# First layer's seven-product projection on one Trainium2 core: sums in the accumulation banks, weight sums on DVE at fixed steps, a written order on every engine, heads turned six steps later

## The chip, the cores and the metric

The kernel runs on one core of a Trainium2 chip. The core has a matrix engine (PE, with its own queue for loading weights, PEld), a vector engine (DVE), an activation engine (ACT), a general-purpose engine (POOL) and a synchronisation engine (SP) from which DMAs are issued; ACT can issue DMAs too. Each engine takes its instructions in the order in which they stand in its queue and waits at semaphores for the others. The metric is the device time of one execution in microseconds (us), less is better.

## What is computed

A two-layer decoder trunk over 1024 tokens of width 1024. The first layer is dilated sliding-window attention, the second a gated linear recurrence; both also attend to 256 memory tokens. The part that matters here is the first layer's input projection, its norms and its rotation:

```python
h = rms_norm(x, norm_gain[l])
cols = h @ w_in_a[j]                       # 1024 tokens x (9 x 1024 + 512 + 1536) columns
qkv = cols.reshape(B, S, 3, N_GROUPS, A_HEADS, HEAD_DIM)
q = rms_norm(qkv[:, :, 0], q_gain[:, None, :])
k = rms_norm(qkv[:, :, 1], k_gain[:, None, :])
v = qkv[:, :, 2]
q = apply_partial_rotary(q, cos5, sin5)    # the first 32 of 128 numbers of a head
k = apply_partial_rotary(k, cos5, sin5)
...
p = jnp.exp(s - m)                         # attention in windows, three dilations
o = jnp.einsum('brchqk,brckhd->brcqhd', p.astype(v.dtype), vc)
```

All of it is float32.

## The kernel before

**Tiling.** The 9 x 1024 columns of q, k and v are nine groups (line 851): for the dilations g = 2, 1, 0 in this order, k, v and q. A group is a product of 1024 tokens by 1024 inputs with 1024 inputs by 1024 columns. It is cut into halves both ways and done with seven products of 512 x 512 x 512 instead of eight (Winograd's form of Strassen's algorithm). The sides made of tokens are the quarters a11, a12, a22 and the sums s1 to s4 (line 852), turned once before and kept as a rounded high part and a rest (`hhi`, `hlo`, `s2hi` and so on). The sides made of weights are the quarters 11, 12, 21, 22 of the group's weights and sums of them.

**A product** (`product`, line 970) has four tiles of 128 tokens by 512 columns. A tile is 12 matmuls: four blocks of inputs, each with high x high, high x low and low x high (lines 983 to 985). Here one such tile is called a step; a group has 28 steps, the stage 252. Before, each tile had its own bank of PSUM (`acc`, three banks, and `po`, one), and all sums over products were made outside: by DVE from bank and SBUF (lines 993, 1000, 1004, 1005, 1008, 1011), one on POOL (line 1001), with copies out of the bank by ACT in three products (line 169).

**Weights.** `load` (line 856) brings halves of a quarter, 512 KB each, into raw tiles; `combine` (line 880) makes the sums in place, six on DVE and two on POOL per group (line 881); `split_side` (line 869) makes the rounded high half on ACT (`wh`) and the rest on DVE (`wl`, line 877), one product ahead, into a ring of four. `weights_ahead` (line 883) says after which tile of which product all this is issued.

**Heads.** A finished tile of q or k (16 per group) holds four heads of 128 tokens. `projected` (line 940): ACT squares it (946), DVE reduces (948) and adds the epsilon (176), POOL takes the power -0.5 (178), DVE scales (950), and POOL rotates (915, 917 twice, 919). Four ticks later (three for one tile) `spill_heads` (line 954) has PE turn the four heads (313), ACT takes them out of the bank with the gain (961), and a DMA on ACT's queue stores them to `qk_scr` (963, 967). Tiles of v are stored as they are.

**Order.** A scheduler orders the instructions of each engine; in this stage `with pinned()` (line 1040) holds PE's in program order, and only PE's. Loads are issued by SP, stores by ACT (line 108).

**Behind the stage** come the gates of the memory columns (`gate_mem`, lines 1088 and 1091), the memory's norm and projections, and the attention. There a loop over heads and tiles does scores, probabilities (DVE and ACT, tile `pa`, three buffers), turns them on PE (1157) and multiplies with the values (1170); a tile is turned one tile after its scores.

## Time and profile before

| | us |
|---|---|
| median of three timed runs | 2260.11 (2257.26, 2260.11, 2260.25) |
| the profiled execution's own time | 2256.34 |
| its span, first to last instruction | 2254.5 |
| busy in the span: PE | 2110.3 |
| DVE | 1307.1 |
| ACT | 852.4 |
| POOL | 596.4 |

TensorE's mean granted clock in the profiled execution is 0.977 of full speed. The profile names an instruction by engine, line of the kernel, operation and tiles (output <- inputs). "Idle before" is the time in which an engine waited just ahead of an instruction, and "<-" names what ended that wait. Busy times are sums over an engine; which of them sets the end is read from a stretch of the span and from who waits for whom. The seven-product stage reaches from the first matmul of line 983 at 73.9 us to about 929 us.

### The profile page before, as it was taken

Reading aid. Unit: us, or ns where it says so; the run is one execution under the profiler, and the core shown is the slowest. Engines: PE = TensorE matmul, PEld = TensorE weight load, DVE = VectorE, ACT = ScalarE, POOL = GpSimd, SP = SyncE. Lnnn points to the kernel's source line nnn. Section 1 sums busy time; section 2 is a strip of 40 time slices with the busy share of each in tenths; the row PEclk is TensorE's granted clock in tenths of the full one; section 3 lists DMA queues with packets and bytes.
Section 4 is the critical chain, followed back from the end, with each engine's and each line's share of the span. In section 5 each row is a group of like instructions: output and inputs, shape, how many; then the busy total and the mean of one; then the engine's idle time right before and its main releaser. Section 6 shows DMA issues by size and latency. Waiting matters only on the chain.

```text
span 2254.5 us, 29624 instructions
## 1 busy us (share of the span) xinstructions
PE 2110.3 (94%) x10713; PEld 1752.2 (78%) x10713; DVE 1307.1 (58%) x2546; ACT 852.4 (38%) x1599; POOL 596.4 (26%) x718
## 2 busy tenths in 40 slices
PE   7899988899888998899879999999999999999999
PEld 5677866778666786678768788888888888888887
DVE  7765557565676656555545755442557772777443
ACT  6544235352353423444655533232542322222211
POOL 2553155541566415402100630001310000000221
PEclk9999999999999999999999999999999999999999
DMA  6465356444343332642677847432111111212633
GB/s 185 122 102 100 112 100 78 98 103 126 84 86 106 109 121 82 208 150 61 212 259 239 269 142 257 151 121 73 57 57 48 57 48 50 73 47 88 221 121 112
DMA packets 416449, 272.50 MB, mean 121 GB/s; under 512 B 220448, under 2 KB 344624, under 8 KB 414256
## 3 DMA queue, kind: packets, MB, share of 16 engines
q1 hardware_dynamic: 155808, 189.72, 27.4%
q10 hardware_dynamic: 260496, 80.89, 14.4%
q8 instruction: 85, 1.39, 0.3%
q14 instruction: 60, 0.49, 0.1%
HBM read 187.60 MB, written 82.97 MB: 120 GB/s over the span
## 4 chain that ended last, share of the span: by engine, by line
PE 71%; DVE 9%; DMA 7%; POOL 5%; ACT 4%; issue 3%; ACTq 1%; SPq 0%; DVEq 0%; POOLq 0%
PE acc L983 6%; PE acc L984 6%; PE acc L985 6%; PE acc L495 5%; PE acc L496 5%; PE acc L497 5%; PE acc L600 4%; PE acc L601 4%; PE acc L602 4%; PE acc L255 4%; PE acc L254 4%; PE acc L253 4%; PE pt L313 2%; POOL rr L178 2%; PE s L1143 1%
## 5 line engine op out<-in xcount | busy, mean ns | idle before, releaser
L178 POOL TENSOR_TENSOR rr<-rv,nhalf 128x4 f32<-128x4 f32 (+1 forms) x150 | 155.8, 1041 | 842.9 <-DVE rv L176 841.8
L169 ACT ACTIVATE wh<-raw 128x1024 fp32r<-128x1024 f32 x206 | 217.0, 1058 | 284.4 <-PE acc L985 76.6
L877 DVE TENSOR_TENSOR wl<-raw,wh 128x1024 fp32r<-128x1024 f32 x126 | 158.1, 1258 | 175.3 <-ACT wh L169 175.2
L983 PE MATMUL acc<-wh,hhi 128*128 128x512 f32 x504 | 208.6, 414 | 0.2 <-ACT x L169 0.2
L984 PE MATMUL acc<-wl,hhi 128*128 128x512 f32 x504 | 201.7, 400 | 1.2 <-DVE wl L877 1.2
L985 PE MATMUL acc<-wh,hlo 128*128 128x512 f32 x504 | 201.0, 399 | 0.0
L496 PE MATMUL acc<-hlo,wh 128*128 128x512 f32 x480 | 191.4, 399 | 0.0
L497 PE MATMUL acc<-hhi,wl 128*128 128x512 f32 x480 | 191.2, 398 | 0.0
L495 PE MATMUL acc<-hhi,wh 128*128 128x512 f32 x480 | 190.1, 396 | 0.0
L215 DVE TENSOR_TENSOR wl<-raw,wh 128x1024 fp32r<-128x1024 f32 x80 | 100.2, 1254 | 119.3 <-ACT wh L169 117.8
L255 PE MATMUL acc<-wh,hlo 128*128 128x512 f32 x384 | 151.3, 395 | 5.8 <-DVE hlo L274 5.8
L253 PE MATMUL acc<-wh,hhi 128*128 128x512 f32 x384 | 150.6, 397 | 0.8 <-ACT wh L169 0.8
L254 PE MATMUL acc<-wl,hhi 128*128 128x512 f32 x384 | 151.2, 394 | 0.0
L600 PE MATMUL acc<-wh,yhi 128*128 128x512 f32 x360 | 144.4, 403 | 0.5 <-ACT yhi L169 0.5
L601 PE MATMUL acc<-wl,yhi 128*128 128x512 f32 x360 | 142.8, 397 | 0.0
L602 PE MATMUL acc<-wh,ylo 128*128 128x512 f32 x360 | 141.5, 398 | 0.0
L983 PEld LDWEIGHTS acc<-wh,hhi 128*128 128x128 f32 x504 | 98.8, 196 | 21.0 <-ACT x L169 2.3
L985 PEld LDWEIGHTS acc<-wh,hlo 128*128 128x128 f32 x504 | 97.9, 194 | 21.6
L984 PEld LDWEIGHTS acc<-wl,hhi 128*128 128x128 f32 x504 | 98.5, 196 | 20.4 <-DVE wl L877 1.6
L1148 ACT ACTIVATE pa<-pa,st 128x128 f32<-128x128 f32 (+1 forms) x192 | 84.5, 441 | 69.8 <-DVE st L1146 33.2
L881 POOL TENSOR_TENSOR raw<-raw 128x1024 f32<-128x1024 f32 x18 | 50.7, 2818 | 208.5 <-DVE raw L881 172.7
L496 PEld LDWEIGHTS acc<-hlo,wh 128*128 128x128 f32 x480 | 90.2, 188 | 16.9
(342 smaller groups left out, 5046.8 us busy)
## 6 DMA issues: line engine op xcount, KB each, us to landing
raw<-in_w_in_a_dram SPq DMA_DIRECT2D x106, 512.0 KB, 3.9
raw<-in_w_in_b_dram SPq DMA_DIRECT2D x40, 512.0 KB, 3.8
o_scr<-os ACTq DMA_DIRECT2D x96, 128.0 KB, 4.7
qk_scr<-c ACTq DMA_DIRECT2D x36, 256.0 KB, 4.1
raw<-in_w_mem_kv_dram SPq DMA_DIRECT2D x16, 512.0 KB, 4.1
kT<-qk_scr SPq DMA_DIRECT2D x8, 1024.0 KB, 5.5
qT<-qk_scr SPq DMA_DIRECT2D x8, 1024.0 KB, 8.7
vv<-v_scr SPq DMA_DIRECT2D x8, 1024.0 KB, 8.3
```

What stands on the lines that cost most here:

```text
L253: T.matmul(ps, hi, wh[:, j, :], start=at == 0, stop=False)
L254: T.matmul(ps, hi, wl[:, j, :], start=False, stop=False)
L255: T.matmul(ps, lo, wh[:, j, :], start=False, stop=at == n - 1)
L495: T.matmul(ps[:], wh[:, k, :], mh, start=k == 0, stop=False)
L496: T.matmul(ps[:], wh[:, k, :], ml, start=False, stop=False)
L497: T.matmul(ps[:], wl[:, k, :], mh, start=False, stop=k == 7)
L600: T.matmul(pss[ch][:], hi[:, k, :], wh[:, j, :], start=first and k == 0, stop=False)
L601: T.matmul(pss[ch][:], hi[:, k, :], wl[:, j, :], start=False, stop=False)
L602: T.matmul(pss[ch][:], lo[:, k, :], wh[:, j, :], start=False, stop=end and k == 3)
L983: T.matmul(flat, hi, wh, start=kt == 0, stop=False)
L984: T.matmul(flat, hi, wl, start=False, stop=False)
L985: T.matmul(flat, lo, wh, start=False, stop=kt == 3)
```

## The change

Seven things are changed.

1. The products stand in another order and add up in the banks: each of a tile's four banks takes products 0, 2, 3 and 4 one upon the other, then products 5 and 6; only product 1 has banks of its own (the two of `pS`). What a later sum needs is copied out between two products (`emptied`).
2. All weight sums are made by DVE, at fixed steps (`sums_`); half of quarter 21 and all of 22 are loaded a second time (`21r`, `22r`).
3. High and low halves of a side are made at separate steps (`split_high`, `split_low`).
4. A tile passes through fixed steps: `emptied` and `spread` one step behind its matmuls, `normed` three, `flip` (PE's transposes) six (`BEHIND`), `spill_heads` seven.
5. `pinned` holds PE, DVE, ACT, POOL and SP in program order. Stores of heads and of v are issued by SP instead of ACT.
6. Tiles have new names: rooms m, u and w, four of each, in place of x, y and c.
7. The last heads are finished between and behind the first gate of the memory columns. In the attention a tile's probabilities are turned two tiles after its scores, with four buffers `pa`.

```diff
-        SIDE = ("a12", "a11", "s1", "s2", "s3", "a22", "s4")
+        SIDE = ("a11", "a12", "s2", "s3", "a22", "s1", "s4")
+        FROM = ("11", "21", "22", "11", "21", "12", "22r")
...
         def combine(gi, out, a, b, h):
-            (G if out == "21'" else V).tensor_tensor(raws[gi, out, h], raws[gi, a, h], raws[gi, b, h], op=OP.subtract)
+            V.tensor_tensor(raws[gi, out, h], raws[gi, a, h], raws[gi, b, h], op=OP.subtract)
...
+            first, second = (1, 0) if p == 0 else (0, 1)
+            sums_ = {(0, 0): ("12", "12", "11", 0), (0, 1): ("12", "12", "11", 1), (0, 2): ("22", "22", "12", 0),
+                     (1, 0): ("22", "22", "12", 1), (1, 3): ("11", "22", "11", 0), (2, 0): ("11", "22", "11", 1),
+                     (2, 3): ("21", "21", "22", 0), (3, 0): ("21r", "21r", "22", 1)}
+            if i in (0, 1):
+                split_high(n + 1, (first, second)[i])
+            if i in (1, 2):
+                split_low(n + 1, (first, second)[i - 1])
+            if (p, i) in sums_:
+                out, a, b, h = sums_[p, i]
+                combine(gi, out, a, b, h)
+            for at, what in (((0, 2), ((0, "22", 1),)), ((2, 2), ((0, "21r", 1),)), ((2, 3), ((1, "11", 0),)),
+                             ((3, 0), ((0, "22r", 0),)), ((3, 1), ((0, "22r", 1),)), ((4, 2), ((1, "11", 1),)),
+                             ((4, 3), ((1, "12", 0), (1, "12", 1), (1, "21", 0))), ((5, 2), ((1, "22", 0),)),
+                             ((5, 3), ((1, "21", 1),))):
...
+        def matmuls(k, hook=None):
+            n, i = divmod(k, 4)
+            p = n % 7
+            if p in (0, 5):
+                banks[i] = bank(i)
+            ps = pS.tile([128, 4, 128], F32, name="s")[:] if p == 1 else banks[i]
...
+                T.matmul(flat, hi, wh, start=kt == 0 and p in (0, 1, 5), stop=False, **on)
+                T.matmul(flat, hi, wl, start=False, stop=False, **on)
+                T.matmul(flat, lo, wh, start=False, stop=kt == 3, **on)
...
+            if p in (0, 2, 3):
+                return
+            Q, m = {1: (0, i), 4: (0, 4 + i), 5: (1, 4 + i), 6: (1, i)}[p]
+            to = (ms, None, None, None, None, vs, us)[p - 1 if p == 1 else p]
+            if p != 4:
+                V.tensor_tensor(to[i], to[i], ps, op=OP.add)
+                c = to[i]
+            else:
+                ms[i] = c = room(f"m{i}")
+                copy(A, c, ps)
+            if i_ == 2:
+                Y.dma_start(tile_of(v_scr[g], m)[:, Q * 512:(Q + 1) * 512], c.rearrange("p h d -> p (h d)"))
+                return
...
+        def step(k, fill=None):
+
+            n, i = divmod(k, 4)
+            if k <= LAST:
+                sums_at[k] = matmuls(k)
+            spill_heads(k - 1 - BEHIND)
+            if k - 1 in sums_at:
+                emptied(k - 1, sums_at.pop(k - 1))
+            normed(k - 3)
+            if k <= LAST:
+                weights_ahead(n, i)
+                if i == 3 and n % 7 == 0 and groups[n // 7][0] != 2:
+                    group_tables(*groups[n // 7])
+            if fill:
+                fill()
+            spread(k - 1)
+            flip(k - BEHIND)
...
+        for k in range(LAST + 1):
+            with pinned(E.PE, E.DVE, E.Activation, E.Pool, E.SP):
+                step(k, {LAST - 2: lambda: ahead(1), LAST - 1: lambda: ahead(2)}.get(k))
...
+        step(LAST + 1)
+        gate_mem(MG0[0], between=lambda: [step(LAST + k) for k in (2, 3, 4)])
+        for k in range(5, BEHIND + 3):
+            step(LAST + k)
...
-                p = ap_.tile([128, 2, 256], F32, name="pa", bufs=3)
+                p = ap_.tile([128, 2, 256], F32, name="pa", bufs=4)
...
-                        old = turn_(*scored.pop()) if scored else None
+                        old = turn_(*scored.pop(0)) if len(scored) > 1 else None
```

Three places show how the instructions move on the engines. The first is DVE at the seam where the fourth group begins (k of the second dilation). `wl` is the low half of a side, `raw` a half of a quarter of the weights, `rc` and `rs` the group's rotation tables, `m`, `u`, `c` and `y` tiles of heads, `rr` the factor of the norm. Before:

```order
L950 TENSOR_TENSOR y3_2463<-y3_2463,rr4_2976 128x512
L924 TENSOR_TENSOR rc_693<-turns_126,gr_125 128x256
L927 SCALAR_TENSOR_TENSOR rs_694<-turns_126,gr_125 128x8x16 x2
L877 TENSOR_TENSOR wl_3124<-raw_2580,wh_3123 128x1024
L881 TENSOR_TENSOR raw_2580<-raw_3018,raw_2580 128x1024
L877 TENSOR_TENSOR wl_3128<-raw_2582,wh_3127 128x1024
L881 TENSOR_TENSOR raw_2490<-raw_2580,raw_2490 128x1024
L993 TENSOR_TENSOR c_3105<-x0_3008,acc_3092 128x512
L881 TENSOR_TENSOR raw_2582<-raw_3020,raw_2582 128x1024
L993 TENSOR_TENSOR c_3144<-x1_3044,acc_3131 128x512
```

and after:

```order
L1008 TENSOR_TENSOR u2_2374<-u2_2374,rr4_2854 128x512
L889 TENSOR_TENSOR wl_2926<-raw_2700,wh_2886 128x1024
L893 TENSOR_TENSOR raw_2562<-raw_2562,raw_2529 128x1024
L1008 TENSOR_TENSOR u3_2398<-u3_2398,rr4_2893 128x512
L889 TENSOR_TENSOR wl_2958<-raw_2564,wh_2924 128x1024
L893 TENSOR_TENSOR raw_2662<-raw_2662,raw_2560 128x1024
L930 TENSOR_TENSOR rc_691<-tabs_124 128x256
L933 SCALAR_TENSOR_TENSOR rs_692<-tabs_124 128x8x16 x2
L893 TENSOR_TENSOR raw_2961<-raw_2961,raw_2562 128x1024
L980 TENSOR_TENSOR m0_2915<-m0_2915,s_2993 128x512
L889 TENSOR_TENSOR wl_3038<-raw_2662,wh_3010 128x1024
```

The new group's sums (L893) and low halves now stand between the last scalings of the group before (L1008), ahead of the tables, where before the sums came behind the last heads of the group before.

The second place is SP's queue around the same seam: loads of `raw` and, after, the stores of heads to `qk_scr`. Before:

```order
L864 DMA raw_3022<-in_w_in_a_dram 128x2x512
L864 DMA raw_2721<-in_w_in_a_dram 128x2x512
L864 DMA raw_2723<-in_w_in_a_dram 128x2x512
L864 DMA raw_3018<-in_w_in_a_dram 128x2x512
L864 DMA raw_3020<-in_w_in_a_dram 128x2x512
```

and after:

```order
L1031 DMA qk_scr02_94<-w3_2481 128x32x16
L869 DMA raw_2961<-in_w_in_a_dram 128x2x512
L1031 DMA qk_scr02_94<-u0_2317 128x32x16
L1031 DMA qk_scr02_94<-u1_2342 128x32x16
L1031 DMA qk_scr02_94<-u2_2374 128x32x16
L1031 DMA qk_scr02_94<-u3_2398 128x32x16
L869 DMA raw_3186<-in_w_in_a_dram 128x2x512
```

The loads of block 22's second half (raw_2961) and of the second copy of 21's (raw_3186) now stand among stores of the group before.

The third place is ACT inside a group of q: squares of tiles of heads (into `s`), turned heads taken out of the bank `pt`, and, before, their stores. Before (q of the second dilation, products 4 to 6):

```order
L961 ACTIVATE c_4790<-pt_4915 128x4x32x4
L967 DMA qk_scr01_93<-c_4790 128x16x32
L946 ACTIVATE s_4900<-os_4897 128x512
L961 ACTIVATE c_4835<-pt_4963 128x4x32x4
L967 DMA qk_scr01_93<-c_4835 128x16x32
L946 ACTIVATE s_4936<-x0_4408 128x512
```

and after (q of the third dilation, products 4 to 6):

```order
L989 ACTIVATE s_2587<-m3_2585 128x512
L172 ACTIVATE wh_2596<-raw_2403 128x1024
L989 ACTIVATE s_2618<-w0_2424 128x512
L172 ACTIVATE wh_2627<-raw_2430 128x1024
L989 ACTIVATE s_2651<-w1_2451 128x512
L1025 ACTIVATE m0_2497<-pt_2670 128x4x16x8
L989 ACTIVATE s_2691<-w2_2467 128x512
L1025 ACTIVATE m1_2523<-pt_2708 128x4x16x8
```

The stores have left ACT's queue, and between a tile's square and its leaving the bank stand six steps instead of three or four: `m0` leaves after the square of `w1`, while before the first `c` left ahead of the square of `os`, the fourth tile of its product.

276 lines of the change are left out of this document (123 added, 153 removed).

## The prediction

> **What bounds the kernel now.** I read the stretches by engine first, then who PE waits for, then the pace of its matmuls. From the page's first line and the table of stretches (us; per engine busy us and instructions; then TensorE's granted clock, DMA share, GB/s):
>
> ```profile
> span 2254.5 us, 29624 instructions
> 74.00:929.00 855.00, 772.39 (x3417) 621.90 (x3416) 526.12 (x703) 335.82 (x426) 395.50 (x529) 0.96 0.44 103
> 1100.00:1300.00 200.00, 173.69 (x1156) 150.88 (x1155) 114.20 (x502) 114.53 (x416) 37.72 (x34) 0.95 0.80 263
> 1300.00:2254.50 954.50, 949.58 (x5064) 803.38 (x5063) 515.48 (x1055) 271.06 (x496) 103.48 (x93) 1.00 0.32 101
> ```
>
> The first stretch is the nine groups of seven products, which the change rewrites; the second is the attention of layer A, where it edits two lines. After 1300 PE is busy 949.6 of 954.5 us, and nothing there changes. So whatever can be won lies in PE's 83 idle us (855.0 - 772.4) of the first stretch and its 26 of the second, and in the clock below 1.00 there. Who PE waits for between 80 and 1000 us (total us, times, longest):
>
> ```profile
> PE pt L313 <- DVE rv L176: 43.1, 6, 7.4
> PE pt L313 <- POOL c L919: 18.4, 13, 3.1
> ```
>
> PE hardly waits for weights; it waits, in program order, in front of a tile's transposes (L313), whose heads are not yet scaled and rotated. The timeline shows PE's pace without such a wait, and after one:
>
> ```profile
> 301.37 0.39 PE L983 MATMUL po<-wh,hhi 128*128 128x512 f32 x1
> 304.10 0.39 PE L983 MATMUL acc<-wh,s2hi 128*128 128x512 f32 x1
> 311.80 0.40 PE L983 MATMUL acc<-wh,s2hi 128*128 128x512 f32 x1
> 326.26 0.40 PE L985 MATMUL po<-wh,s3lo 128*128 128x512 f32 x1
> 329.57 1.12 PE L313 MATMUL pt<-ident,c 128*128 128x128 f32 x4 [2.91 <-POOL c L919]
> 330.91 0.63 PE L984 MATMUL acc<-wl,hhi 128*128 128x512 f32 x1
> 331.34 0.63 PE L985 MATMUL acc<-wh,hlo 128*128 128x512 f32 x1
> 334.31 0.60 PE L313 MATMUL pt<-ident,c 128*128 128x128 f32 x4
> 334.67 0.48 PE L983 MATMUL acc<-wh,hhi 128*128 128x512 f32 x1
> 334.99 0.39 PE L984 MATMUL acc<-wl,hhi 128*128 128x512 f32 x1
> ```
>
> A step (one tile of one product, 12 matmuls) takes 304.10 - 301.37 = 2.73 us with a side from hhi, and 12 x (311.80 - 304.10)/33 = 2.80 us with a summed side. Four transposes add 0.45 us: the second matmul behind them starts at 334.99 instead of 334.31 + 0.23. After an idle gap of 2.91 us matmuls start 0.43 us apart, not 0.23: a wait costs more than its own length.
>
> **The floor of this stage.** Of 252 steps 144 have an hhi side and 108 a summed one, before and after: 144 x 2.73 + 108 x 2.80 = 695.5 us, and 96 tiles of q and k are turned: 43.2. That is 739 us. Measured are 855, of which some 13 matmuls of the gate behind the stage take 3: an excess of 113 us. The three v groups turn no heads, so it lies in the six q and k groups, about 19 us each: some 103 us a group instead of 84.5.
>
> **The change part by part.** The durations (min/median/max in ns for the first rows; count, busy us and mean ns for the last five), from the lines and groups of this stage:
>
> ```profile
> L877 DVE TENSOR_TENSOR wl<-raw,wh x126: 1210/1225/2316, 71.6 to 898.2; 128x1024 fp32r<-128x1024 f32 x126
> L881 DVE TENSOR_TENSOR raw<-raw x54: 1210/1225/3424, 83.5 to 848.8; 128x1024 f32<-128x1024 f32 x54
> L881 POOL TENSOR_TENSOR raw<-raw x18: 2361/2822/3313, 88.8 to 857.9; 128x1024 f32<-128x1024 f32 x18
> L950 DVE TENSOR_TENSOR c<-c,rr x36: 679/693/941, 100.7 to 900.5; 128x512 f32<-128x512 f32 x36
> L948 DVE TENSOR_REDUCE ss<-s x96: 676/684/693, 96.6 to 931.9; 128x4 f32<-128x512 f32 x96
> L176 DVE TENSOR_SCALAR rv<-ss x150: 138/164/555, 5.7 to 2106.5; 128x4 f32<-128x4 f32 x132, 128x1 f32<-128x1 f32 x18
> L178 POOL TENSOR_TENSOR rr<-rv,nhalf x150: 550/1011/2050, 6.0 to 2109.5; 128x4 f32<-128x4 f32 x132, 128x1 f32<-128x1 f32 x18
> L915 POOL TENSOR_TENSOR t<-c,rc x36: 446/460/789, 101.6 to 901.3; 128x128 f32<-128x128 f32 x36
> L917 POOL TENSOR_TENSOR t<-x,rs x48: 311/320/330, 159.7 to 919.4; 128x64 f32<-128x64 f32 x48
> L919 POOL TENSOR_TENSOR c<-t,t x36: 451/458/1433, 104.1 to 903.2; 128x128 f32<-128x128 f32 x36
> L1001 POOL TENSOR_TENSOR y<-y,x 128x512 f32<-128x512 f32 x36 | 54.7, 1523 | 125.6 <-DVE x L1000 110.0 <-issue 15.6
> L1008 DVE TENSOR_TENSOR x<-x,acc 128x512 f32<-128x512 f32 x32 | 21.8, 682 | 12.1 <-PE acc L985 12.0
> L169 ACT ACTIVATE wh<-raw 128x1024 fp32r<-128x1024 f32 x126 | 132.5, 1057 | 174.8 <-PE acc L985 76.6 <-PE po L985 64.3 <-issue 24.9
> L169 ACT ACTIVATE x<-acc 128x512 f32<-128x512 f32 x63 | 37.7, 599 | 108.3 <-DVE c L993 65.6 <-PE acc L985 31.7 <-DVE wl L877 4.8
> L961 ACT ACTIVATE c<-pt,gqk 128x512 f32<-128x512 f32 x18 | 18.3, 1015 | 27.1 <-PE pt L313 24.2 <-POOL t L917 2.9
> ```
>
> *Sums in the banks.* A group's 24 DVE additions become 12 (0.68 us each: 8 us less DVE); POOL loses four additions (4 x 1.5) and two weight sums (2 x 2.8), 12 us. DVE gains those two sums (2.5 us), ACT four copies out of a bank (2.4 us). PE's matmuls stay the same in number. A q or k group then asks of DVE 14 x 1.23 (low halves) + 8 x 1.23 (sums) + 12 x 0.68 + 16 x (0.69 + 0.68 + 0.16) = 60 us, of POOL 16 x (1.01 + 0.46 + 2 x 0.32 + 0.46) = 41, of ACT 14 x 1.06 + 32 x 0.60 + 16 x 1.02 = 50. PE needs 84.5. No engine is the bound by its sum.
>
> *New waits on the banks.* A bank is read one step after its product and written again four or more steps later: at least three steps, 8.2 us, cover a read of 0.6 to 0.7. The second product uses two other banks in turn, so there the addition must be done within the next step, 2.7 us. Cost nothing, unless DVE runs more than about 2 us late there.
>
> *Heads turned six steps behind.* From the end of a tile's matmuls its chain is addition 0.68, square 0.60, reduction 0.68, 0.16, power 1.01, scaling 0.69, rotation 1.56: 5.4 us. Between the tile and its transposes now stand five whole steps, 13.7 us at the least. The waits of 43.1 and 18.4 us go as long as DVE and POOL are less than 8 us behind. What is late next is DVE at the seam of two groups. From the sixth product's second step to the next group's third, ten steps, DVE has scalings, low halves and three sums on top of POOL's rotations.
>
> *DVE against POOL.* Two neighbours of the timeline show how much they exclude each other:
>
> ```profile
> 88.78 3.31 POOL L881 TENSOR_TENSOR raw<-raw 128x1024 f32<-128x1024 f32 x1 [10.88 <-DVE raw L881]
> 89.75 3.42 DVE L881 TENSOR_TENSOR raw<-raw 128x1024 f32<-128x1024 f32 x1
> 366.20 1.00 POOL L178 TENSOR_TENSOR rr<-rv,nhalf 128x4 f32<-128x4 f32 x1
> 366.30 1.21 DVE L877 TENSOR_TENSOR wl<-raw,wh 128x1024 fp32r<-128x1024 f32 x1
> ```
>
> DVE's sum took 3.42 us instead of 1.23 until POOL's had ended, but a low half issued inside a power took 1.21. So long POOL operations hold DVE up, powers don't. Over those ten steps scalings and rotations (10 x 2.25), four low halves with p = 5, 6 and two more with p = 0 (6 x 1.23) and three sums (3.7) make 33.6 us one after the other, where PE takes 31.6 (one step of 2.73, five of 2.73 + 0.45, four of 2.80 + 0.45). The 2 us are within the step or so by which low halves are made ahead. I put 2 us per q or k group, 12 in all, and bound it by 0 and by the 10 of the rival below.
>
> The Trainium skill, page "SBUF — State Buffer", section "SBUF: two separate sides", says that a DVE operation with two SBUF inputs and a POOL operation exclude each other for the whole instruction. The first pair agrees; the second, 1.21 us beside a power, does not. By the rule for all of POOL the sum would be the first rival's 2195, by the rows it is 2155.
>
> *Stores move from ACT's queue to SP's, and weights are loaded again.* Eleven loads of 512 KB per group instead of ten; the stores of heads now stand between them. Issue to landing (us, min/median/max), the first row for the weights, the second for qk_scr:
>
> ```profile
> DMA to landing us min/median/max: 3.5/3.9/8.8
> DMA to landing us min/median/max: 2.2/4.8/11.8
> ```
>
> Nearly all loads are issued four or more steps before their sum. Two are tight: block 22's second half, issued at the first product's third step behind a store, is summed some 5 us later (two steps of 3.2 less the 1.0 of ACT's scaling in front of that store); the reload of 21's is as close. A landing up to about 10 us only uses DVE's reserve; the usual one is 3.9, or 3.9 + 4.8 = 8.7 behind a store. Cost: 0, bounded by (11.8 - 10) x 12 = 22 us. A room is written again six steps after its store is issued, 16 us against a longest landing of 11.8: nothing.
>
> The Trainium skill, page "DMA: Bandwidth & Descriptors", section "Queues, rings and completion order", has one ring per issuing engine and turns taken between rings, so that a load now starts behind a store's descriptors instead of beside them. That speaks against this part: by it landings near 8.7 become the rule and DVE's reserve is used up at every seam, by the rows above they are the exception. No trace here shows it yet.
>
> *Attention, two tiles behind instead of one.*
>
> ```profile
> PE pt L1157 <- ACT pa L1148: 25.1, 24, 4.4
> 1123.69 8.50 DMA o_scr<-os
> ```
>
> PE waited 25.1 us for probabilities between 1085 and 1300 us. A tile takes about 2.1 us (200 us for some 96), so one tile more of distance removes a wait up to that length; the longer ones follow transfers in the chain, such as this of 8.50 us, and are only postponed. Between 0 and 25 I take 10. Start and end of the stage (first splits, last heads) I leave at 8 us of excess, between 0 and 20: the last heads still meet the memory's load and its norm.
>
> **The sum.** Excess 113 becomes 12 + 8 = 20: 93 us less. With 10 from attention 103. Against the profiled execution's own 2256.3 us that is 2153. The three timed runs have a median of 2260.1, 0.17% more, so I round up to 2155. With the bounds (excess from 0 to 45, which is twice the 12, and 20 for start and end; attention from 25 to 0) this case alone spans 2118 to 2188; nearest to its rows, 2138 to 2175.
>
> **Rivals.** *Powers hold DVE too, or DVE in program order falls behind at the seam.* Eight powers within the ten steps make 33.6 into 41.7 us against 31.6; 4 us of reserve leave 6 per group, 36, and the slow matmuls after each gap bring it to some 40: 2195. For it: the 43.1 us in front of transposes all came from a DVE that was held up. Against it: the 1.21 us.
>
> *Loads queue behind stores; slower.* Only if the two tight loads of six groups land L us after issue, with 12 x (L - 10) above 103, does it decide: L over 18.6. At L = 20 it gives 2155 + 120 = 2275. Against it: no landing above 11.8 us, and DMA at a share of 0.44. It keeps its 0.06 since no row shows loads and stores in one queue.
>
> *Little comes of it.* Program order on every engine ties each step to a DVE addition, an ACT square and a POOL power; if DVE's 60 us and POOL's 41 then simply follow each other, a q or k group takes 101 us instead of 103. Excess 6 x 16.5 + 8 = 107: 2240 with attention's 10, 2250 without, so on both sides of what can be told. Against it: powers and reductions overlap the other engine in the rows above.
>
> **Chances.** Forecast 0.72, first rival 0.16, slower 0.06, little 0.06. The range 2130 to 2210 holds the forecast and the first rival, and leaves out the last two and some 0.06 of the tails. Faster by over 0.2% (about what a measurement of this kernel can tell from no change): 0.72 + 0.16 + half of the little case, 0.91; within 0.2%, its other half, 0.03; slower 0.06.
>
> **What would show it.** Right: in the stage PE's idle time below 25 us, its clock at 1.00 in nearly all slices, no waits of PE's transposes on rv; a q or k group at 85 to 88 us. Rows of DVE sums of 3.4 us are gone. Wrong: waits of PE for low halves (wl) at the start of groups (first rival), or DVE sums waiting for raw loads by over 10 us (second). If attention keeps its 25 us behind ACT, its term is wrong alone.

## The result and the profile after

The changed kernel takes 2114.86 us (median of four runs, 2114.33 to 2117.12) against 2260.18 (2257.26 to 2260.36): a ratio of 0.9362, 95% interval 0.9346 to 0.9378. The prediction had 2155 in a range of 2130 to 2210: the sign and the place were right, and the gain was taken too small, by a quarter of the 139 us by which the profiled spans differ.

First line and stretches of the changed kernel's profile, columns as before:

```profile
span 2115.3 us, 29553 instructions
74.00:809.60 735.60, 730.65 (x3380) 603.57 (x3380) 459.00 (x619) 343.62 (x454) 316.92 (x458) 1.00 0.54 121
809.60:981.00 171.40, 157.19 (x838) 131.99 (x838) 98.86 (x190) 90.44 (x185) 44.55 (x54) 0.98 0.47 146
981.00:1181.00 200.00, 181.60 (x1278) 164.41 (x1277) 127.96 (x564) 125.13 (x461) 49.90 (x43) 0.97 0.87 282
```

In the seven-product stage PE is idle for 5 of 735.6 us (83 of 855 before), at a clock of 1.00. Who PE still waits for there and in the memory part (first fence), and in the attention (second; us in total, times, longest):

```profile
PE acc L957 <- DVE wl L889: 4.5, 1, 4.5
PE acc L956 <- ACT wh L172: 1.6, 1, 1.6
PE pt L299 <- DVE rv L179: 6.6, 1, 6.6
```

```profile
PE po L1208 <- ACT os L172: 8.8, 5, 2.9
PE pt L1195 <- ACT pa L1186: 5.8, 5, 2.4
```

No transposes of heads are in the list any more. What is left are the first weight halves of the stage (L956, L957; most of the 1.6 us lies ahead of 74.0), the memory's norm (L299) and the attention's own chain. Where the time went is read from the first and last start of three groups of PE, before (lines 1143, 1157, 1170) and after:

```profile
L1143 PE MATMUL s<-kT,qT x384: 270/379/634, 1094.4 to 1316.0; 128*128 128x128 f32 x104, 128*128 128x256 f32 x88
L1157 PE MATMUL pt<-ident,pa x280: 270/273/476, 1096.5 to 1322.5; 128*128 128x128 f32 x140
L1170 PE MATMUL po<-vv,pts x288: 270/275/433, 1101.3 to 1342.0; 128*128 128x128 f32 x144
L1181 PE MATMUL s<-kT,qT x384: 271/275/421, 979.9 to 1179.6; 128*128 128x128 f32 x104, 128*128 128x256 f32 x88
L1195 PE MATMUL pt<-ident,pa x280: 272/273/475, 981.7 to 1194.0; 128*128 128x128 f32 x140
L1208 PE MATMUL po<-vv,pts x288: 270/275/582, 986.0 to 1206.7; 128*128 128x128 f32 x144
```

| part of the span | before | after | measured | predicted |
|---|---|---|---|---|
| stage | 855.0 | 735.6 | -119.4 | -93 |
| memory part, to the first scores | 165.4 | 170.3 | +4.9 | 0 |
| attention, first scores to last transposes | 228.1 | 214.1 | -14.0 | -10 |
| from there to the last values | 19.5 | 12.7 | -6.8 | 0 |
| rest | 912.5 | 908.6 | -3.9 | 0 |
| sum | | | -139.2 | -103 |

The first two rows share a piece of work: before, 19 matmuls of the gate (920.9 to 925.2 us) stood within the stage, and now they stand behind it with the transposes of three tiles more. PE does 829 instructions in the memory part instead of 794, so its 4.9 us are moved work and no new wait.

One thing in these profiles was in no theory. The timeline shows the pace of matmuls with a summed side (start and duration in us; 27 matmuls lie between the two starts):

```profile
186.52 0.39 PE L956 MATMUL acc<-wh,s2hi 128*128 128x512 f32 x1
192.64 0.39 PE L956 MATMUL acc<-wh,s2hi 128*128 128x512 f32 x1
```

That is (192.64 - 186.52)/27 = 0.2267 us, so 2.72 us for a step, where the prediction read 2.80 before and took it for a property of the summed side. The floor of the stage is then 252 x 2.72 + 43.2 = 728.6 us instead of 739, and the excess above it 7 instead of 20. In the diff one line had been passed over: the spacer tile `left` shrinks from 40 to 32 numbers, 160 to 128 bytes. In the program's layout `s2hi` starts at byte 132128 of a partition before (32 past a multiple of 64) and at 131840 after (a multiple of 64); the other sums, one room each of `qT` and `kT`, and the second layer's sides moved in the same way, while `hhi` did not move.

### The profile page after: what moved, and what is told of

The parts are those of the page before. It is cut to its first block, busy times and chain, and to the rows that moved or that the text cites. A ratio compares the mean times of both kernels' runs of the same rounds, so it can differ in the third digit from the quotient of the medians.

```text
span 2115.3 us, 29553 instructions
## 1 busy us (share of the span) xinstructions
PE 2054.5 (97%) x10713; PEld 1733.5 (82%) x10713; DVE 1242.4 (59%) x2457; ACT 863.1 (41%) x1635; POOL 533.6 (25%) x664
## 4 chain that ended last, share of the span: by engine, by line
PE 46%; DMA 5%; ACT 1%; DVE 1%; issue 0%; ACTq 0%; POOL 0%; SPq 0%; DVEq 0%
PE acc L498 5%; PE acc L499 5%; PE acc L500 5%; PE acc L603 4%; PE acc L604 4%; PE acc L605 4%; PE acc L258 3%; PE acc L256 3%; PE acc L257 3%; DMA o_scr<-os 3%; PE s L1404 1%; PE pt L1404 1%; PE s L1181 1%; PE po L1208 1%; ACT pa L1186 1%; PE pt L299 1%
## 5 line engine op out<-in xcount | busy, mean ns | idle before, releaser
L181 POOL TENSOR_TENSOR rr<-rv,nhalf 128x4 f32<-128x4 f32 (+1 forms) x54 | 50.0, 926 | 759.4 <-DVE rv L179 750.9
L1001 POOL TENSOR_TENSOR rr<-rv,nhalf 128x4 f32<-128x4 f32 x96 | 125.0, 1302 | 412.2 <-DVE rv L999 411.0
L258 PE MATMUL acc<-wh,hlo 128*128 128x512 f32 x384 | 151.0, 394 | 4.9 <-DVE hlo L277 4.9
L256 PE MATMUL acc<-wh,hhi 128*128 128x512 f32 x384 | 150.4, 396 | 1.5 <-ACT wh L172 0.9
L257 PE MATMUL acc<-wl,hhi 128*128 128x512 f32 x384 | 151.0, 393 | 0.0
L957 PE MATMUL acc<-wl,hhi 128*128 128x512 f32 x324 | 127.0, 392 | 4.5 <-DVE wl L889 4.5
L956 PE MATMUL acc<-wh,hhi 128*128 128x512 f32 x324 | 128.1, 395 | 1.6 <-ACT wh L172 1.6
L958 PE MATMUL acc<-wh,hlo 128*128 128x512 f32 x324 | 127.0, 392 | 0.0
L498 PEld LDWEIGHTS acc<-hhi,wh 128*128 128x128 f32 x480 | 90.3, 188 | 18.3 <-ACT wh L172 1.6
L500 PEld LDWEIGHTS acc<-hhi,wl 128*128 128x128 f32 x480 | 90.3, 188 | 16.8 <-DVE wl L218 0.3
L893 DVE TENSOR_TENSOR raw<-raw 128x1024 f32<-128x1024 f32 x72 | 90.2, 1260 | 16.4 <-DMA raw<-in_w_in_a_dram 16.4
```

Source lines behind the costliest of these rows:

```text
L256: T.matmul(ps, hi, wh[:, j, :], start=at == 0, stop=False)
L257: T.matmul(ps, hi, wl[:, j, :], start=False, stop=False)
L258: T.matmul(ps, lo, wh[:, j, :], start=False, stop=at == n - 1)
L498: T.matmul(ps[:], wh[:, k, :], mh, start=k == 0, stop=False)
L500: T.matmul(ps[:], wl[:, k, :], mh, start=False, stop=k == 7)
L956: T.matmul(flat, hi, wh, start=kt == 0 and p in (0, 1, 5), stop=False, **on)
```

## The experiments

"Before" is the median of the kernel before in the same session; the ratio is to it, with its 95% interval. The last column is read from each run's one trace: from the start of the seven products' first matmul to the start of their last. It is 854.3 us in the kernel before and 734.8 in the changed one.

| run | what it is | median us (range) | before | ratio | stage us |
|---|---|---|---|---|---|
| e1_shift32 | changed kernel, addresses moved back | 2121.7 (2119.5 to 2126.0) | 2256.6 | 0.9393 (0.9351 to 0.9436) | 739.6 |
| e2_before_aligned | before, addresses alone | 2249.1 (2236.0 to 2259.7) | 2256.6 | 0.9962 (0.9937 to 0.9987) | 857.7 |
| e3_attention_one | changed, attention undone | 2132.3 (2127.6 to 2135.3) | 2256.6 | 0.9441 (0.9404 to 0.9479) | 734.7 |
| e4_pe_order_only | changed, only PE ordered | 2127.2 (2125.7 to 2130.3) | 2256.6 | 0.9423 (0.9387 to 0.9459) | 750.6 |
| e5_behind4 | changed, four steps | 2134.3 (2131.6 to 2136.9) | 2257.5 | 0.9451 (0.9427 to 0.9475) | 750.7 |
| e6_pool_sums | changed, two sums on POOL | 2115.5 (2109.8 to 2119.1) | 2257.5 | 0.9366 (0.9339 to 0.9393) | 734.9 |
| e7_stores_act | changed, stores on ACT | 2113.1 (2110.7 to 2117.0) | 2257.5 | 0.9357 (0.9328 to 0.9386) | 734.7 |
| e8_sums_outside | changed, no sums in banks | 2117.4 (2116.2 to 2119.7) | 2257.5 | 0.9377 (0.9355 to 0.9400) | 737.4 |
| e9_behind4_pe_order | e4 and e5 together | 2139.7 (2134.1 to 2141.3) | 2260.6 | 0.9461 (0.9440 to 0.9483) | 768.5 |
| e10_parts_undone | e4 to e8 together | 2177.6 (2172.1 to 2181.1) | 2260.6 | 0.9631 (0.9607 to 0.9655) | 804.7 |
| e11_before_ordered | before, all engines ordered | 2330.3 (2325.7 to 2331.0) | 2260.6 | 1.0303 (1.0278 to 1.0327) | 928.1 |
| e12_dve_sums_alone | before, all sums on DVE | 2249.5 (2246.9 to 2257.6) | 2258.9 | 0.9965 (0.9945 to 0.9985) | 853.6 |
| e13_before_six | before, six steps | 2179.6 (2170.4 to 2184.5) | 2260.6 | 0.9638 (0.9608 to 0.9667) | 771.3 |
| e14_three_edits | e13, addresses, attention | 2136.5 (2135.7 to 2138.3) | 2257.2 | 0.9456 (0.9428 to 0.9484) | 759.7 |
| e16_four_edits | e14, all sums on DVE | 2125.9 (2120.9 to 2129.0) | 2257.2 | 0.9408 (0.9380 to 0.9436) | 749.9 |
| e17_seven_steps | e16 with seven steps | 2109.9 (2108.8 to 2114.9) | 2258.9 | 0.9349 (0.9326 to 0.9371) | 735.2 |
| after_again | the changed kernel | 2113.6 (2110.0 to 2116.2) | 2257.2 | 0.9355 (0.9329 to 0.9380) | 734.8 |
| e15_better | changed, two edits more | 2114.8 (2109.3 to 2119.3) | 2257.2 | 0.9360 (0.9329 to 0.9391) | 735.6 |

Below, "over the changed kernel" is counted from 2114, between its two medians. The intervals reach 4 to 10 us to either side, so the times alone don't tell a few us from nothing; there the stage column, which is the same in both traces of the changed kernel, says more.

### The addresses

```diff
-    small.tile([128, 32], F32, name="left", bufs=1)
+    small.tile([128, 24], F32, name="left", bufs=1)
```

> The changed kernel, only with the spacer tile `left` of 24 instead of 32 numbers, so that the tiles behind it (s2hi to s4lo, qT and kT, the later yhi, ylo, mhi) start 32 bytes past a multiple of 64 again, as before the change. Theory A (the start address of PE's sides sets 2.80 against 2.72 us for a step with a summed side): 108 x 0.08 = 8.7 us come back in the stage, its matmuls from s2hi again 0.233 us apart (rows of 395 ns instead of 389), and some 4 to 8 us behind it (the 3.9 us of the part after the attention, and some in the memory part); total 2115 + 13, between 2123 and 2135. Rival (the pace came from DVE and POOL disturbing PE's reads less in the new order): pace stays 0.227, total within 3 us of the changed kernel's.

```diff
-    small.tile([128, 40], F32, name="left", bufs=1)
+    small.tile([128, 32], F32, name="left", bufs=1)
```

> The kernel before, only with `left` of 32 numbers, so that the same tiles start at multiples of 64 bytes. Theory A: rows of its summed-side matmuls at 389 ns instead of 395, pace 0.227 us; in the three v groups and behind the stage the gain is kept, in the q and k groups part of it turns into longer waits in front of the transposes: 5 to 17 us less, 2243 to 2255. Rival (pace from the order of DVE and POOL): no change, within 3 us of 2260.

One group of matmuls (ns, min/median/max) in the kernel before, in before with the spacer changed, in the changed kernel, and in the changed kernel with the spacer moved by 32 bytes, in this order:

```profile
L983 PE MATMUL acc<-wh,s2hi x128: 392/395/396, 119.9 to 883.8; 128*128 128x512 f32 x128
L983 PE MATMUL acc<-wh,s2hi x128: 388/389/500, 120.0 to 887.7; 128*128 128x512 f32 x128
L956 PE MATMUL acc<-wh,s2hi x108: 389/389/389, 102.6 to 758.1; 128*128 128x512 f32 x108
L956 PE MATMUL acc<-wh,s2hi x108: 392/395/398, 102.6 to 763.0; 128*128 128x512 f32 x108
```

And the pace in the last of the four, 27 matmuls again:

```profile
186.90 0.40 PE L956 MATMUL acc<-wh,s2hi 128*128 128x512 f32 x1
193.20 0.40 PE L956 MATMUL acc<-wh,s2hi 128*128 128x512 f32 x1
```

(193.20 - 186.90)/27 = 0.2333 us, the pace of before. The row follows the address both ways and not the order of the other engines, so the rival falls. Worth: 8 us over the changed kernel, and 7.5 us in the kernel before. The first is below the 13 expected; the span grows by 8.9 in the profiled runs, 4.8 of it ahead of the first scores (984.7 us instead of 979.9), where 8.7 were expected for the stage alone, and 4.8 behind the attention. The traced execution of e2 is the slowest of its ten; it gains 4.9 us behind the attention and nothing in the stage, whose q and k groups still wait for heads.

### The attention

```diff
-                p = ap_.tile([128, 2, 256], F32, name="pa", bufs=4)
+                p = ap_.tile([128, 2, 256], F32, name="pa", bufs=3)
...
-                        old = turn_(*scored.pop(0)) if len(scored) > 1 else None
+                        old = turn_(*scored.pop()) if scored else None
```

> The changed kernel with the attention's two edits undone (probabilities turned one tile behind, three buffers pa). Prediction's term: 10 us slower (bounds 0 and 25). The comparison of the traces has the attention 14.0 us shorter up to its last scores and transposes and 6.8 behind them: 14 to 21 us slower, and PE's waits for pa back near 25 us. Rival (the attention gained from what comes before it, such as free transfers or the addresses): under 5 us.

18 us over the changed kernel, and in its trace PE waits for probabilities as before:

```profile
PE pt L1195 <- ACT pa L1186: 27.5, 21, 4.7
```

The predicted mechanism, nearly twice its 10 us; no wait for `os` is left in this trace. The sum had counted only the wait for probabilities. The 6.8 us of the table's fourth row come back too: the last values start at 1226.5 us, 19.3 behind the last transposes (1207.2).

### Parts of the stage undone one at a time

```diff
-            with pinned(E.PE, E.DVE, E.Activation, E.Pool, E.SP):
+            with pinned():
```

> The changed kernel with only PE held in program order in the stage, DVE, ACT, POOL and SP ordered by the scheduler as before. If the sums in the banks and the distance of six steps do the work: within 5 us of 2115, PE's idle time in the stage below 15 us. Rival (the written order is what keeps DVE and POOL from running late): waits of PE for rv, for low halves or for the turned tile return, 20 to 90 us slower.

```diff
-BEHIND = 6
+BEHIND = 4
```

> The changed kernel with BEHIND = 4: heads are turned four steps behind their tile, the distance of the kernel before, all else as changed. If the distance removed the waits in front of the transposes (43 + 18 us and more before), a large part of them comes back: 40 us or more. If the written order and the lighter DVE and POOL removed them, the chain (scaling at the third step, rotation done 2 to 3 us later) still ends before the transposes of the fourth: within 5 us of 2115, and only single waits below 1.5 us.

```diff
-            V.tensor_tensor(raws[gi, out, h], raws[gi, a, h], raws[gi, b, h], op=OP.subtract)
+            (G if out in ("21", "21r") else V).tensor_tensor(raws[gi, out, h], raws[gi, a, h], raws[gi, b, h], op=OP.subtract)
```

> The changed kernel with the two weight sums from the quarter 21 (21 and 21r) on POOL again, as before. If two-input operations of DVE and POOL excluding each other (rows of 3.42 us) made the waits of before: such rows return and PE waits 20 us or more in the stage. If six steps of distance and a written order take that up: rows near 3 us return on DVE, but PE's waits stay below 12 us and the time within 5 us of 2115.

```diff
-                Y.dma_start(qk_scr[i_][g][:, 4 * Q:4 * Q + 4, m * 128:(m + 1) * 128], o)
+                SQ.dma_start(qk_scr[i_][g][:, 4 * Q:4 * Q + 4, m * 128:(m + 1) * 128], o)
```

(and in the same way the stores of g = 1, 2 and of v)

> The changed kernel with the stores of heads and of v issued by ACT again. Prediction's second rival had loads late behind stores in SP's queue; the trace of after has DVE wait 16.4 us for raw tiles and PE for none of it. If the queue cost nothing: within 3 us of 2115, DVE's wait for raw tiles shorter, ACT a little later. If SP's queue was a cost or ACT's issuing one: over 5 us faster or slower.

```diff
-            if p in (0, 5):
+            if p != 1:
                 banks[i] = bank(i)
...
-                copy(A, us[i], ps)
+                V.tensor_tensor(us[i], us[i], ps, op=OP.add)
             elif p == 3:
                 vs[i] = room(f"w{i}")
-                copy(A, vs[i], ps)
+                V.tensor_tensor(vs[i], us[i], ps, op=OP.add)
...
+            if p == 1:
+                us[i] = room(f"u{i}")
+                copy(A, us[i], ms[i])
+            if p == 5:
+                V.tensor_tensor(us[i], us[i], ps, op=OP.add)
...
-                copy(A, c, ps)
+                V.tensor_tensor(c, vs[i], ps, op=OP.add)
```

> The changed kernel with the sums over products made outside the banks again: each product starts its bank anew, DVE adds bank and SBUF (28 additions a group instead of 12, that is 16 x 0.68 = 10.9 us more DVE a group; ACT 8 copies out of banks less). By the prediction's sums DVE then has 71 us of work in a q or k group of 84, still no bound: 0 to 15 us slower, waits of PE for DVE's additions (m, u, w) in small pieces. Rival (the sums in the banks are what won the time): 50 us or more slower.

Over the changed kernel: 13 us for the order, 20 for the distance, 1 for POOL's sums, -1 for the stores, 3 for the sums outside the banks. The distance cost less than the 40 expected and more than the 5; the order more than 5 and less than 20. So neither theory had either size, and the last three can't be told from nothing by the time (in the stage they are 0.1, -0.1 and 2.6 us). With four steps PE waits again, briefly; the stage grows by 15.9 us, 12.6 of it in these waits, and the memory part behind it by 5.8:

```profile
PE pt L316 <- POOL m L925: 9.3, 6, 1.8
PE pt L316 <- POOL u L925: 3.3, 5, 0.7
```

With only PE ordered the stage grows by 15.8 us. PE waits for rotated tiles, and for DVE's additions in the two banks of the second product, which the prediction had put at nothing unless DVE runs late there:

```profile
PE pt L316 <- POOL u L925: 5.9, 7, 1.6
PE s L956 <- DVE m L980: 5.4, 5, 1.1
```

With POOL's sums back, DVE's long rows are back (third number), and no wait of PE's transposes with them:

```profile
L893 DVE TENSOR_TENSOR raw<-raw x54: 1211/1218/3327, 79.0 to 750.9; 128x1024 f32<-128x1024 f32 x54
L893 POOL TENSOR_TENSOR raw<-raw x18: 2392/2400/2408, 112.5 to 762.8; 128x1024 f32<-128x1024 f32 x18
```

The stores on ACT change the landing of the weights from the first row to the second, in the median by 0.6 us, and nothing in the time:

```profile
DMA to landing us min/median/max: 3.5/4.4/8.6
DMA to landing us min/median/max: 3.3/3.8/11.9
```

### Undone together

The next kernel has the edits of e4 and e5, the one after it those of e4 to e8.

> The changed kernel with both BEHIND = 4 and only PE in program order. Alone the two cost 19 and 12 us. If they are separate prices: 30 to 35 us slower than the changed kernel, 2145 to 2150. If each covers for the other (a late DVE matters only where the distance is short): 60 us or more slower, with waits of PE's transposes for rv and for the rotated tile above 40 us in sum.

> The changed kernel with every part of the stage undone that was tried alone: four steps of distance, only PE in program order, the two sums from 21 on POOL, stores on ACT, sums over products outside the banks. If these parts make the stage's gain and only hide each other: near the kernel before less the attention (18) and the addresses (9), 2215 to 2240. If the gain sits in what is left of the change (the order of the products, weight sums and splits at fixed steps, a tile's chain cut into steps): 2150 to 2185.

Distance and order together cost 26 us where they sum to 33 alone; in the stage they cost 33.7 and sum to 31.7. Within the intervals these are separate prices: the two do not cover for each other. All five together cost 64, where they sum to 37 alone (in the stage 69.9 and 34.3): POOL's sums, the stores and the sums outside the banks, worth 4 us with six steps and a written order, cost 38 with four steps and a free one. PE's waits there:

```profile
PE pt L316 <- POOL w L925: 26.2, 5, 6.3
PE pt L316 <- POOL u L925: 10.4, 12, 1.9
PE pt L316 <- POOL m L925: 8.5, 8, 2.5
```

The time falls in the range of the second forecast: 49.6 us of the stage (804.7 against 854.3 before) stay won by what is left of the change. Which part of it does this (the order of the products, the fixed steps, the chain cut into steps, the addresses) was not tried apart in this kernel. Measured by undoing, then, the distance looks like 20 of the stage's 119 us. That is misleading, as the next runs show.

### Parts alone in the kernel before

```diff
-                projected(i_, g, 0, i, c, 4 if i < 3 else 3)
+                projected(i_, g, 0, i, c, 6)
```

(the other three calls likewise; the second product's fourth tile is kept in `os` instead of `y3`)

> The kernel before with heads turned six steps behind their tile instead of four (the second product's fourth tile kept in another room for it). If the distance is the cure by itself: most of the 61 us of waits of PE for rv and c, and the slow matmuls after them, go: 2170 to 2215. If DVE, ordered by the scheduler, is late by more than two steps at the seams, or stays the bound in a q or k group: 2235 or more, the waits for rv still there.

```diff
-            with pinned():
+            with pinned(E.PE, E.DVE, E.Activation, E.Pool, E.SP):
                 product(n, (lambda i, h: ahead(3 + h) if i == 3 else ahead(2)) if n == last else None)
```

> The kernel before with all five engines held in program order in the stage. There a tile's whole chain (square, reduction, power, scaling, rotation) stands in one piece behind its matmuls, so DVE, in order, waits some 2 us for ACT's square and POOL's power in 16 tiles of six groups: up to 190 us more DVE time of which PE sees what exceeds its 84 us a group: 2260 to 2400, slower. Rival (the written order alone is a gain, whatever the text's order): 2250 or less.

```diff
-            (G if out == "21'" else V).tensor_tensor(raws[gi, out, h], raws[gi, a, h], raws[gi, b, h], op=OP.subtract)
+            V.tensor_tensor(raws[gi, out, h], raws[gi, a, h], raws[gi, b, h], op=OP.subtract)
```

> The kernel before with all weight sums on DVE and nothing else. If POOL's sums (2.8 us each, DVE held up to 3.42) are what makes DVE late at the seams: the waits for rv (43 us) shrink by half or more, 2200 to 2235. If the distance of four steps is short anyway: the gain is that seen with six steps (10 us) or less, 2245 to 2260.

Two steps of distance, alone, bring 81 us (83.0 in the stage of its trace, which is of the fastest of its four executions): most of the stage's gain, in a kernel that still adds outside the banks, has POOL make weight sums and leaves four engines to the scheduler. The waits for rv are gone, these are left:

```profile
PE pt L313 <- POOL c L919: 22.9, 12, 3.8
```

Why two steps are enough is seen in the kernel before at the second product's first tile of the third group (timeline, all engines, in order of time):

```profile
273.07 3.26 POOL L881 TENSOR_TENSOR raw<-raw 128x1024 f32<-128x1024 f32 x1 [42.73 <-DVE raw L881]
273.99 3.42 DVE L881 TENSOR_TENSOR raw<-raw 128x1024 f32<-128x1024 f32 x1
277.33 0.67 DVE L993 TENSOR_TENSOR c<-x,acc 128x512 f32<-128x512 f32 x1
...
284.90 0.69 DVE L950 TENSOR_TENSOR c<-c,rr 128x512 f32<-128x512 f32 x1 [0.30 <-POOL rr L178]
...
288.33 0.46 POOL L919 TENSOR_TENSOR c<-t,t 128x128 f32<-128x128 f32 x1
288.84 1.11 PE L313 MATMUL pt<-ident,c 128*128 128x128 f32 x4 [7.07 <-DVE rv L176]
```

DVE comes to the addition some 4 us late (the tile's last matmul starts at 272.95), held by a weight sum that POOL's own sum stretches; the scaling stands behind other tiles' work; the rotated tile is ready at 288.33 + 0.46 = 288.79, and PE starts at 288.84. (The wait is put down to rv, which came last by the semaphores; the rotation on POOL is what ended there.) PE had waited 7.07 us: two steps and two sets of transposes, 6.4 us, take nearly all of that. The stretched sum is 2.2 us of the lateness (3.42 instead of 1.22), and e12, which takes it away, keeps the waits: it is the length of the chain that four steps do not hold.

Program order for all engines, alone, makes the kernel before 70 us slower. With a tile's chain in one piece DVE stands waiting for POOL's power and ACT's square again and again:

```profile
DVE c L952 <- POOL rr L180: 40.5, 36, 1.1
DVE ss L950 <- ACT s L948: 60.3, 71, 1.2
```

(28.4 us in 14 pieces and 33.4 in 28 in the kernel before.) In these two kernels the order is a gain only where the chain is cut into steps. All sums on DVE, alone, give 9 us; PE's waits for rv stay (46.1 us, six times), as the second theory had it.

### Put together

The next has e13's edits, `left` of 32 numbers and the change's two attention edits; the one after it all sums on DVE too; the third seven steps instead of six.

> The kernel before with three small edits only: heads turned six steps behind (as e13_before_six), `left` of 32 numbers, attention two tiles behind with four buffers pa. If the parts add up: 81 + 18 + 9 = 108 us faster than before, 2150 to 2156. If the addresses gain more now that PE no longer waits in the q and k groups: down to 2145. Rival (they share a cause, such as the slow matmuls after a gap): 2165 or more.

> The kernel before with the same three edits and all weight sums on DVE. If the rows of 3.42 us (DVE held up by POOL's sums) make the waits for c that six steps leave (22.9 us, 12 times, and slow matmuls after each): those waits go, 2118 to 2130, so that four small edits reach the changed kernel nearly. Rival (the rest of the gain needs the new order of products and steps): within 5 us of e14_three_edits.

> The four small edits of e16_four_edits with seven steps of distance instead of six. If the waits left (12.1 us for c, six times, one at each q or k group, and the slow matmuls behind them) are lateness of one step: they go, 2110 to 2118, as fast as the changed kernel. If they come from a tile whose rotation is ordered late by the scheduler whatever the distance: 2122 or more.

> The changed kernel once more, as the standard for the others on this chip: 2110 to 2120, ratio 0.934 to 0.940.

Three small edits: 121 us, 13 more than the parts in sum and below all three forecasts; by the profiled spans (2168.6 and 2136.5) addresses and attention add 32 where 27 were expected, so that part of the surplus is the spread of e13's runs. The stage is 11.6 us shorter than e13's, more than the 4.8 of e1; why the addresses give more here is not shown. All sums on DVE: 11 more. One step more: 16 more by the medians, which are of two sessions, 13 by the ratios. What PE still waits for in front of the heads' transposes, with six steps and with seven:

```profile
PE pt L313 <- POOL c L919: 12.1, 6, 2.8
PE pt L313 <- POOL c L919: 4.3, 6, 1.8
```

With that the kernel before, with these four edits and one step more, stands at 2109.9 us, ratio 0.9349 (0.9326 to 0.9371), against 0.9355 (0.9329 to 0.9380) for the changed kernel on the same scale: the two can't be told apart. Its stage:

```profile
73.00:808.00 735.00, 729.59 (x3380) 601.40 (x3380) 522.14 (x714) 330.18 (x421) 366.20 (x499) 1.00 0.51 118
```

735 us, as in the changed kernel, with 63 us more DVE and 49 more POOL work in it, all hidden.

### An attempt to go further

```diff
-                tables()
                 s0.close()
...
             keep_s1(j)
+        tables()
...
-                os = ap_.tile([128, 4, 128], F32, name="os")
+                os = ap_.tile([128, 4, 128], F32, name="ot", bufs=3)
                 copy(A, os[:], o[:])
```

> The changed kernel with two more edits: the rotation tables are made behind the last gate product instead of ahead of it, so that DVE makes the first low half earlier (PE waits 4.5 us for it), and the attention's spilled tiles have three rooms of their own (ACT waits 10.9 us for stores of os, PE 8.8 us for ACT's os). Both waits gone: 8 to 13 us faster than the changed kernel, 2102 to 2107. Rival (the tables are then late for the first rotations, or the waits in the attention pass to the next in the chain, pa): within 3 us, or slower.

No change: 2114.8 us. Its waits in the two places:

```profile
PE acc L957 <- DVE wl L889: 4.9, 1, 4.9
PE po L1208 <- ACT ot L172: 3.5, 2, 1.9
PE pt L1195 <- ACT pa L1186: 9.1, 5, 3.2
```

The first low half is as late as it was, so moving the tables' place in the text did not move them out of its way; and in the attention the wait went on to pa (5.8 us in the changed kernel's first trace), as the rival had it.

## Why the prediction was right or wrong

- **What bounds the kernel:** right. PE waited in front of transposes for heads that were late, not for weights, and each wait cost more than its length: 83 idle us in an excess of 113.
- **Heads turned six steps behind:** right, and the main term. The "less than 8 us behind" is borne out: in the changed kernel the second product's first tile of the fourth group, whose transposes waited 7.44 us before, is rotated at 347.90 and turned at 354.74 (rows below), 6.8 us to spare. The tightest tile of the stage has 3.8.

```profile
344.66 0.69 DVE L1008 TENSOR_TENSOR m<-m,rr 128x512 f32<-128x512 f32 x1
345.43 1.38 POOL L921 TENSOR_TENSOR t<-m,rc 128x128 f32<-128x128 f32 x1 [0.53 <-DVE m L1008]
347.44 0.46 POOL L925 TENSOR_TENSOR m<-t,t 128x128 f32<-128x128 f32 x1
354.74 0.60 PE L316 MATMUL pt<-ident,m 128*128 128x128 f32 x4
```

- **"What is late next is DVE at the seam of two groups", 12 us:** wrong, and this is the step that failed. The sum of 33.6 us took DVE's and POOL's work of ten steps as one row of work. In the changed kernel the two lie beside each other: in the same ten steps at the seam of the third and fourth group (row below; PE, PEld, DVE, ACT, POOL) DVE is busy for 29.5 us and POOL for 29.9, both within PE's 31.4, and PE does not wait. The sum also left out DVE's additions and reductions, which those 29.5 us hold. In e6, with POOL's sums back, no wait appears either; in e8, with 16 more additions a group, PE waits 2.7 us more.

```profile
299.98:331.40 31.42, 31.42 (x157) 25.96 (x156) 29.51 (x43) 18.60 (x23) 29.85 (x46) 1.00 0.97 95
```

- **The floor of 739 us:** wrong by 10, if the pace of 0.2267 us holds throughout. The 2.80 us were the address of the sides, not the sides. The rows of both e1 and e2 show it; of its size e1 shows 4.8 us in the stage, where its wait for the first low half is also 1.6 us shorter. The change of `left` had no term in the sum, and neither had the 3.9 us behind the attention: in every trace with the old addresses that last stretch takes 912.5 to 913.4 us, in every one with the new ones 906.7 to 908.6.
- **Start and end, 8 us:** nearly right in the stage (excess 7, of which 4.5 are the wait for the first low half); the 4.9 us of the memory part, which had no term, are the gate matmuls and transposes that left the stage.
- **Attention, 10 of 25 us:** right mechanism, too small. Of the 25.1 us 19.3 went, new waits for os took back 8.8, and the end got 6.8 us shorter: 20.8 by the spans, 18 by e3.
- **Sums in the banks, new waits on them, stores on SP:** put at about nothing for the time, and so measured (3, 0 and -1 us); waits on the second product's banks appear only in e4 (5.4 us) and e8 (2.0). That no engine is the bound by its sum is what e8 and e17 confirm.
- **DVE against POOL:** the rows of 3.42 us are real, but their price was not on PE's path once the distance was there (e6). The Trainium skill, page "SBUF — State Buffer", section "SBUF: two separate sides", would have a DVE operation with two SBUF inputs and a POOL operation that reads SBUF exclude each other for the whole instruction, whichever starts first. For two-input sums the measurement bears this out: DVE's rows reach 3.33 us with POOL's sums in e6, and 1.48 without them in the changed kernel (first row). For POOL's power it holds one way only. In the changed kernel's trace DVE issued 40 sums and low halves inside a power, and none took more than 1.23 us; but 13 powers issued inside such an operation took 1.9 to 2.0 us instead of 1.0 (one pair below). In the rows above, too, it is POOL that is slow: a rotation product of 0.46 us took 1.38 beside a weight sum of DVE.

```profile
L893 DVE TENSOR_TENSOR raw<-raw x72: 1211/1221/1480, 80.8 to 760.9; 128x1024 f32<-128x1024 f32 x72
107.23 1.48 DVE L889 TENSOR_TENSOR wl<-raw,wh 128x1024 fp32r<-128x1024 f32 x1
107.58 2.00 POOL L1001 TENSOR_TENSOR rr<-rv,nhalf 128x4 f32<-128x4 f32 x1
```

- **Rivals:** powers holding DVE did not happen, and loads behind stores landed only 0.6 us later in the median (e7). The waits that "Little comes of it" feared from program order are those of e11, the order without the steps; the change has the steps.

So 36 us were missing from the forecast: 13 in the seam and the rest of the excess, 10 in the floor, 11 in the attention and 4 behind it, less 2 between gate matmuls that no longer lie within the stage (3 by the prediction's count of 13; the trace has 19, 4.3 us) and the memory part (5). The forecast's own bounds reached down to 2118, and the range was cut at 2130: both were built on the floor of 739, which was itself too high.

## What to carry to other kernels

Where an engine waits in program order for the end of a chain, first count the chain's length in steps and lengthen the distance: that is one number, and here it was two thirds of what a rewrite of the stage brought. Parts of a rewrite that look worthless when each is undone alone may be hiding each other, and the part that looks small may be most of the gain when it is done alone; do both, undo in the new kernel and add in the old. Read every line of a diff that changes a tile's size, since all addresses behind it move.

## What the hardware showed that was not expected

A 128x512 matmul starts every 0.2333 us instead of 0.2267 when its side of tokens, the one that is loaded as weights, starts 32 bytes past a multiple of 64 (rows of 395 and 389 ns; the rows of the weight loads themselves stay at 188 ns). It is 3% of such matmuls and was about 8 us of this kernel. Matmuls with `hhi`, whose address did not change, have 389 ns in both kernels; other offsets than 32 were not tried, and why the address matters stays open. The Trainium skill, page "SBUF — State Buffer", section "Operand start alignment", asks for multiples of the element's size only and says that this is about legality, not speed; what the rows show is a price in speed that it does not give.
